# Attention of a trunk layer: full-row low products, inverse sums by two products, four heads' values together

## The chip, the cores and the metric

The kernel runs on one core of a Trainium2 chip. The metric is the device time of one execution in microseconds (us), as a median of runs. TensorE is called PE here (its weight loads PEld), VectorE DVE, ScalarE ACT, GpSimd POOL, SyncE SP.

## What is computed

The reference is a two-layer trunk for 512 latent tokens and 256 context tokens of 1024 features, followed by a second, larger block. The change touches only the attention of the trunk's layers: eight query heads of 64 features share two key and value heads, four query heads each. Cut to what matters here:

```python
def gqa_attend(qb, k, v):
    s = jnp.einsum('bqhgd,bkhd->bhgqk', qb, k, preferred_element_type=jnp.float32) * HEAD_DIM ** -0.5
    p = jax.nn.softmax(s, axis=-1)
    return jnp.einsum('bhgqk,bkhd->bqhgd', p.astype(v.dtype), v)

def trunk_layer(...):
    qc_, kc_, vc_ = attn_qkv(aqc, akc, avc, g_q, g_k)        # context: 256 tokens
    ql, kl, vl = attn_qkv(aq, ak, av, g_q, g_k)              # latent: 512 tokens
    k_all = jnp.concatenate([kc_, kl], axis=1)
    v_all = jnp.concatenate([vc_, vl], axis=1)
    ... latent_attention(ql, k_all, v_all) ...               # both layers
    ... context_attention(qc_, kc_, vc_) ...                 # first layer only
```

## The kernel before

Everything is float32. The large products run as three passes over float32r operands: each operand is split into a high part and a low rest, and high times high, high times low and low times high are added up in PSUM (`mm3`, L293 to L297). Weights stream in by SP's queue, and ACT, DVE and POOL make their two parts (L282, L284, L285).

The order of all instructions is set when the program is built: the kernel is written as straight code, and a scheduler of the framework interleaves it per engine by a timeline that it simulates. Each engine then runs its list in that order and waits on semaphores.

Attention is run three times: for the context in the first layer (4 blocks of 128 queries and four heads), and for the latent tokens in both layers (8 such blocks each). `keys` normalises the keys, turns them feature-major with PE and writes them into one tile `K`: the high parts of the two key heads on all 128 partitions (each head's 64 features twice, one copy above the other), and the low part of a head on one half of the partitions only (L871). `attend` then takes one head of one block after the other:

- `queries` (once a block): scaled and turned queries, four transposes into the bank `at`, then a tile `q` that holds the high part on one half of the partitions and the low part on the other (L920, L921).
- `scores`: for each set of keys a product on all 128 rows with the keys' high parts (L929), so that high and low part of the query are both covered, then a product on the 64 rows of the query's high half with the keys' low part (L930), and a maximum (L931). For the latent tokens there are two sets, 512 keys (bank `SL`) and 256 keys (bank `SC`), so two products on 64 rows for each head; for the context one set.
- `weights`: exponentials with their sums (L944), transposes of 128 columns each into `at` or the right half of the bank `op` (L947), copies to `PT` (L250 and L252).
- `values`, after every second head: products with 64 columns of the values, so that one head's result lies on the upper half of the partitions and the other's on the lower (L956). After the fourth head also the reciprocal of the sums (L962), four products that spread the inverse sums over 64 partitions each (L965, into `at`), a copy (L968) and two multiplications that write the output and free `op` (L970).

A float32 product shows as two records in the trace, a float32r product as one. Beside attention PE runs other work in the same stretches: the projections and the context's MLP (L295 to L297), the gated linear attention (`gla_out`, L705 to L744), pieces of the modulation (L450).

Of the kernel before, what the change touches and what calls it, by code (L numbers as in the profile page):

```python
# [7 lines left out]
LAG = 1  # L8
# [15 lines left out]
# groups of 256 columns of the scan's convolved part: keys, queries and values of two of its groups at a time  # L24
# [3 lines left out]
# ---------------------------------------------------------------- host side: layout and shape constants  # L28
# [5 lines left out]
def _pack(w, cols, kb=4):  # L34
    """[K, N] -> groups of 1024 rows and cols columns, each in contiguous loads of [128, kb*cols]."""
    K, N = w.shape
    return np.ascontiguousarray(
        w.reshape(K // 1024, 8 // kb, kb, 128, N // cols, cols).transpose(0, 4, 1, 3, 2, 5)
    ).reshape(-1, 128, kb * cols)


class Pieces:
    """Tiles side by side, sliced as one piece of memory; no slice reaches over an end."""
# [28 lines left out]
def _bands():  # L72
    """Windowed mean minus the token itself, as matrices over [token in, token out]."""
# [118 lines left out]
# ---------------------------------------------------------------- the kernel  # L192
class Kern:
    SHARED = {"const", "wraw", "whi", "wlo", "mod", "gs", "nv", "nr"} | {f"V{i}" for i in range(8)}
    # work space: tag -> count, of [128, 512]
    WORK1 = dict(E=2, K=2, Q=2, AT=1, QE=1, q=2, d=1, ab=1)
    WORK2 = dict(fa=3, fr=2, fu=2, fy=2, gG=3, gk=2, gm=2, dv=2, dk=2, dq=2, da=2, dn=2, dd=2, jy=2)
    # the tags of a normalisation's square, variance, root and product
# [21 lines left out]
    def w(self, tag, n=512, dt=F32):  # L220
        """Work space [128, n]."""
# [21 lines left out]
    # -- small helpers  # L243
# [12 lines left out]
    def split(self, src, hi, lo, f=None):  # L256
        """src = hi + lo exactly, both in float32r."""
        nc = self.nc
        nc.scalar.activation(hi, src, AF.Copy)
        nc.vector.tensor_tensor(lo, src, hi.bitcast(F32), op=ALU.subtract)  # L260

    def rsqrt(self, v, out, tmp):
        """out = v ** -0.5 of few columns: a first value from the exponent's bits and Newton's steps. v is kept."""
# [9 lines left out]
    # -- weights  # L273
    def whalf(self, name, i, n, kb, soon=True):
        """One load of a packed weight: its two float32r parts, [128, kb, n / kb]."""
# [12 lines left out]
    def wload(self, name, g, soon=True):  # L288
        """A group of 1024 rows and 256 columns, as a function of the block of rows."""
# [9 lines left out]
    def dense(self, name, groups, h, n, consume, halves=(0, 1), soon=True):  # L299
        """out^T [128 features, n tokens] per block of 128 columns of the weight; h per block of its rows."""  # L300
# [15 lines left out]
    def tokens(self, name, g, h, ntb, consume):  # L316
        """out [128 tokens, 256] for pairs of token blocks."""
# [13 lines left out]
    # -- parts of the tokens  # L331
    def parts(self, n, split=1):
        """Halves of the latent tokens, so that one half's normalisation runs beside the other half's products."""
# [3 lines left out]
    def cut(self, blocks, s):  # L337
        """A part of the tokens of blocks, or of pairs of blocks."""
        return [tuple(p[:, s] for p in b) if isinstance(b, tuple) else b[:, s] for b in blocks]

    def dense_parts(self, name, groups, h, n, consume, before, after, halves=(0, 1)):
        """As dense, with the first and the last groups done for one part of the tokens after the other."""
# [8 lines left out]
    # -- normalisation over features, feature-major  # L351
    def bank(self, n):
        """A bank of the work's own, outside the dense products' rotation."""
# [3 lines left out]
    def squares(self, x, n, tags, gains=None):  # L357
        """Means over the features of the squares of x, plus epsilon: token-major columns [128, n / 128]. With gains
        [128, 8, 2], as second columns the means of the squares times those."""
# [27 lines left out]
        # EPS v + mean: the second norm's variance over the first one's factor  # L387
# [4 lines left out]
    def root(self, v):  # L392
        """v ** -0.5"""
# [4 lines left out]
    def spread(self, r):  # L398
        """Columns [128 tokens, blocks] as a row over all partitions, [128, tokens]."""
# [7 lines left out]
    def norm_mod(self, x, n, gs, sh, hs, tags):  # L407
        """hs: pairs that take the two parts of the normalised blocks."""
# [12 lines left out]
    # -- modulation vectors  # L421
    def conditions(self, a, b):
        """silu of two vectors: [128, 8, 32], two columns and zeros."""
# [10 lines left out]
    def modulation(self, name, st, bias, part, bank="mm"):  # L434
        """One of the six vectors, feature-major [128, 8, 2] for both conditions: left to be done a piece at a time
        between other products. Four blocks of rows at a time, each in its own 32 columns of the array."""
# [32 lines left out]
    def flush(self):  # L469
        """Ends the pieces that were begun."""  # L470
# [3 lines left out]
    def modulation_v(self, name, st, bias, part, first=0):  # L474
        """The same for the first condition alone, by the vector engine."""
# [20 lines left out]
    def tick(self, n=1):  # L496
        """Does the next pieces of what was left for later."""
# [6 lines left out]
    def gain(self, mod, j, g):  # L504
        """(1 + scale) * gain for condition j."""
# [17 lines left out]
    def after(self, a, tile):  # L523
        """Has the loads into a tile wait for an array: they would take the place of more urgent ones."""
# [10 lines left out]
    # -- one layer of the first block  # L535
    def area(self, tag, w=8192):
        """A piece of memory, cut up by take()."""
        return self.t([128, w], tag)
# [4 lines left out]
    def blocks(self):  # L543
        """Eight blocks of [128, 512]: the latent residual, or others in its place."""
        return [self.t([128, 512], f"V{i}") for i in range(8)]

    def hpairs(self):
        """Eight pairs of [128, 512] in the three pieces that take a layer's input."""
# [7 lines left out]
    def ground(self):  # L556
        """The layer's larger arrays."""
        return Pieces([self.area("U0", 3072), self.area("U1", 2048), self.area("U2", 2048), self.area("U3", 1024)])

    def keep(self, out):  # L560
        """Takes token-major blocks as they are."""
# [5 lines left out]
    def dup(self, out, scale):  # L567
        """Takes token-major blocks of four heads and turns them feature-major, twice over the partitions."""
# [15 lines left out]
    def gla_proj(self, l, h, n, o):  # L584
        nc = self.nc
        # four blocks of rows at a time, each in its own 32 columns of the array; the gates' product adds them up
# [28 lines left out]
    # -- gated linear attention, both directions: partitions 0-63 forward, 64-127 backward  # L615
# [1304 lines left out]
```

## Time and profile before

| | |
|---|---|
| Median of 3 runs | 3656.49 us (3649.99 to 3657.73) |
| Span of the profiled execution, first to last instruction | 3646.2 us |
| PE busy in the span | 3414.7 us, 94% |
| DVE, ACT, POOL busy | 60%, 40%, 44% |
| Mean granted clock of PE | 0.956 of full |

The profiled execution has no time of its own beside its span; the median of the three timed runs lies 10.3 us above that span. Busy time of PE counts overlapping records once, and the ends of its records are modelled, so the pace of PE is read from the start of one product to the start of the next. A granted clock of 1.0 means 2.4 GHz, 0.5 means 1.2 GHz.

### The profile page before, as it was taken

How to read it: one execution, taken by the hardware profiler on the slowest of the kernel's cores; microseconds unless marked ns; L12 is line 12 of the kernel's file. 1: busy time of each engine (PE TensorE's matmuls, PEld its weight loads, DVE VectorE, ACT ScalarE, POOL GpSimd, SP SyncE). 2: the span in 40 equal slices, each digit the busy share in tenths (PEclk: the TensorE clock that was granted, in tenths of full speed). 3: DMA queues.
4: the chain of work that ended last, by engine and by line, in shares of the span. 5: the costliest groups of instructions: out<-in, count | busy, mean ns of one | idle time of the engine just before them, and what ended most of it. 6: DMA issues, size and time to landing. Idle time of an engine off the chain costs nothing. (4 is left out here: it accounts for less than half of the span.)

```text
span 3646.2 us, 55656 instructions
## 1 busy us (share of the span) xinstructions
PE 3414.7 (94%) x20714; PEld 2833.3 (78%) x20714; DVE 2174.3 (60%) x3724; ACT 1466.0 (40%) x2587; POOL 1601.3 (44%) x1370
## 2 busy tenths in 40 slices
PE   7999999989999999999999998998899998989998
PEld 5777788877788787677788776787898776788886
DVE  4844877457533358755633789768757767564233
ACT  4522765453222255632223655554233323254222
POOL 2522465542343235422344555446445545555433
PEclk9898999999999999999999999999999999989999
DMA  6344124635522220045522364456366666454222
GB/s 224 116 143 137 44 74 140 213 117 162 174 99 98 94 70 22 10 134 189 188 95 91 120 195 131 153 159 191 124 186 203 196 201 184 144 167 145 94 97 75
DMA packets 268414, 492.67 MB, mean 135 GB/s; under 512 B 44912, under 2 KB 129904, under 8 KB 267888
## 3 DMA queue, kind: packets, MB, share of 16 engines
q1 hardware_dynamic: 214128, 447.17, 38.3%
q10 hardware_dynamic: 54016, 41.95, 3.5%
q8 instruction: 163, 2.67, 0.3%
q14 instruction: 107, 0.88, 0.1%
HBM read 431.22 MB, written 57.80 MB: 134 GB/s over the span
## 5 line engine op out<-in xcount | busy, mean ns | idle before, releaser
L285 POOL TENSOR_TENSOR wlo<-wraw,whi 128x384 fp32r<-128x384 f32 (+1 forms) x503 | 736.1, 1464 | 1265.2 <-ACT whi L282 1178.0
L295 PE MATMUL mm<-h,whi 128*128 128x512 f32 (+1 forms) x2344 | 865.3, 372 | 38.1 <-ACT h L418 7.4
L282 ACT ACTIVATE whi<-wraw 128x1024 fp32r<-128x1024 f32 x503 | 530.9, 1056 | 866.2 <-PE mm L296 648.2
L296 PE MATMUL mm<-h,whi 128*128 128x512 f32 (+1 forms) x2344 | 857.6, 366 | 14.2 <-DVE h L419 11.7
L284 DVE TENSOR_TENSOR wlo<-wraw,whi 128x640 fp32r<-128x640 f32 (+1 forms) x503 | 481.7, 958 | 636.3 <-ACT whi L282 629.8
L297 PE MATMUL mm<-h,wlo 128*128 128x512 f32 (+1 forms) x2344 | 841.0, 365 | 6.0 <-DVE wlo L284 5.9
L295 PEld LDWEIGHTS mm<-h,whi 128*128 128x128 f32 x2344 | 448.7, 192 | 124.2 <-ACT whi L282 11.5
L296 PEld LDWEIGHTS mm<-h,whi 128*128 128x128 f32 x2344 | 449.8, 192 | 93.4 <-DVE h L419 20.9
L297 PEld LDWEIGHTS mm<-h,wlo 128*128 128x128 f32 x2344 | 448.4, 192 | 80.7 <-DVE wlo L284 8.8
L296 PE MATMUL mm<-wlo,h 128*128 128x256 f32 x1200 | 353.5, 296 | 32.5 <-DVE wlo L284 27.7
L295 PE MATMUL mm<-whi,h 128*128 128x256 f32 x1200 | 353.2, 297 | 10.7 <-ACT whi L282 9.8
L297 PE MATMUL mm<-whi,h 128*128 128x256 f32 x1200 | 350.0, 293 | 0.0
L296 PEld LDWEIGHTS mm<-wlo,h 128*128 128x128 f32 x1200 | 235.2, 196 | 43.1 <-DVE wlo L284 32.5
L295 PEld LDWEIGHTS mm<-whi,h 128*128 128x128 f32 x1200 | 234.7, 197 | 27.7 <-ACT whi L282 12.5
L297 PEld LDWEIGHTS mm<-whi,h 128*128 128x128 f32 x1200 | 235.2, 196 | 17.2 <-issue 13.7
L295 PE MATMUL mm<-U,whi 128*128 128x512 f32 (+1 forms) x608 | 228.6, 379 | 5.8 <-DVE V L1080 5.8
L296 PE MATMUL mm<-U,whi 128*128 128x512 f32 (+1 forms) x608 | 227.5, 376 | 0.9 <-DVE U L260 0.9
L297 PE MATMUL mm<-U,wlo 128*128 128x512 f32 (+1 forms) x608 | 223.6, 376 | 0.0
L487 DVE SCALAR_TENSOR_TENSOR AT<-mraw,cst,AT 128x512 f32<-128x512 f32 x140 | 119.2, 851 | 88.6 <-DMA mraw<-in_w_ada 52.7
L295 PE MATMUL mm<-big,whi 128*128 128x512 f32 x384 | 155.0, 405 | 5.6 <-ACT whi L282 2.3
L296 PE MATMUL mm<-big,whi 128*128 128x512 f32 x384 | 153.6, 400 | 0.0
L297 PE MATMUL mm<-big,wlo 128*128 128x512 f32 x384 | 150.9, 401 | 0.0
(580 smaller groups left out, 5980.3 us busy)
## 6 DMA issues: line engine op xcount, KB each, us to landing
wraw<-in_w_in SPq DMA_DIRECT2D x166, 512.0 KB, 3.5
wraw<-in_w_up SPq DMA_DIRECT2D x96, 512.0 KB, 3.3
wraw<-in_w_down SPq DMA_DIRECT2D x96, 512.0 KB, 3.3
mraw<-in_w_mod SPq DMA_DIRECT2D x96, 256.0 KB, 3.0
mraw<-in_w_ada SPq DMA_DIRECT2D x96, 256.0 KB, 2.8
wraw<-in_w_out SPq DMA_DIRECT2D x40, 512.0 KB, 3.3
wraw<-in_w_mlp_up SPq DMA_DIRECT2D x40, 512.0 KB, 3.3
mraw<-in_w_late SPq DMA_DIRECT2D x64, 256.0 KB, 2.8
```

The costliest lines, as they stand in the source:

```text
L282: nc.scalar.activation(hi, raw, AF.Copy)
L284: nc.vector.tensor_tensor(lo[:, :c], raw[:, :c], hi[:, :c].bitcast(F32), op=ALU.subtract)
L285: nc.gpsimd.tensor_tensor(lo[:, c:], raw[:, c:], hi[:, c:].bitcast(F32), op=ALU.subtract)
L295: nc.tensor.matmul(out, lh, rh, start=start, stop=False)
L296: nc.tensor.matmul(out, lh, rl, start=False, stop=False)
L297: nc.tensor.matmul(out, ll, rh, start=False, stop=stop)
L487: nc.vector.scalar_tensor_tensor(acc, raw, st[:, k, 0:1], acc, op0=ALU.mult, op1=ALU.add)
```

## The change

Four edits in `keys` and `attend`, and one in how the program is set up:

1. `K` has four slots instead of three. The low parts of both key heads are now written on all 128 partitions by one subtraction of [128, 2, 256] in place of two of [64, 256].
2. The product with the keys' low part runs on all 128 rows. It thus adds the product of the query's low part with the keys' low part too.
3. `values` is called once a block, after the fourth head, for all four heads. `PT` has six buffers instead of three, since four heads' turned exponentials are now held.
4. The inverse sums are first spread by ACT into a tile [128, 4, 64]; then two products with 128 columns take the place of four with 64.
5. The scratch memory set aside for dynamic DMAs is 1024 bytes.

```diff
-        K = self.t([128, 3, n], f"K{n}", 1, F32R)
+        K = self.t([128, 4, n], f"K{n}", 1, F32R)
...
-                for g in range(2):
-                    s = slice(g * 64, g * 64 + 64)
-                    nc.vector.tensor_tensor(K[s, 2, t], tp[s, g], K[s, g, t].bitcast(F32), op=ALU.subtract)
-        return [(K[:, g], K[g * 64:g * 64 + 64, 2]) for g in range(2)], [x[:, 128:] for x in o["kv"]]
+                nc.vector.tensor_tensor(K[:, 2:, t], tp, K[:, :2, t].bitcast(F32), op=ALU.subtract)
+        return [(K[:, g], K[:, 2 + g]) for g in range(2)], [x[:, 128:] for x in o["kv"]]
...
-            his, qh = halves(g)[0], q[:, hh * 128:(hh + 1) * 128]
+            qh = q[:, hh * 128:(hh + 1) * 128]
             for i, (kk, _, c) in reversed(list(enumerate(ksets))):
                 hi, lo = kk[g]
                 nc.tensor.matmul(at[i], qh, hi, start=True, stop=False)
-                nc.tensor.matmul(at[i], qh[his], lo, start=False, stop=True)
+                nc.tensor.matmul(at[i], qh, lo, start=False, stop=True)
...
-            pt = self.t([128, 768], "PT", 3)[:, :nk]
+            pt = self.t([128, 768], "PT", 6)[:, :nk]
...
-        def values(g, qb, pr, x, pts, op):
-            for b, v in enumerate(vals):
-                for j in range(2):
-                    nc.tensor.matmul(op[j * 64:j * 64 + 64, pr * 128:(pr + 1) * 128], v[:, g * 64:(g + 1) * 64],
-                                     pts[j][:, b * 128:(b + 1) * 128], start=(b == 0), stop=(b == len(vals) - 1))
-            if pr == 0:
-                return
+        def values(g, qb, x, pts, op):
+            for pr in range(2):
+                for b, v in enumerate(vals):
+                    for j in range(2):
+                        nc.tensor.matmul(op[j * 64:j * 64 + 64, pr * 128:(pr + 1) * 128], v[:, g * 64:(g + 1) * 64],
+                                         pts[pr * 2 + j][:, b * 128:(b + 1) * 128], start=(b == 0),
+                                         stop=(b == len(vals) - 1))
...
-            for h in range(4):
-                nc.tensor.matmul(r[h % 2 * 64:h % 2 * 64 + 64, h // 2 * 128:(h // 2 + 1) * 128],
-                                 x[:, 4, h:h + 1].to_broadcast([128, 64]), self.ident, start=True, stop=True)
+            inv = self.t([128, 4, 64], "inv")
+            nc.scalar.activation(inv, x[:, 4].unsqueeze(2).to_broadcast([128, 4, 64]), AF.Copy)
+            for i in range(2):
+                nc.tensor.matmul(r[:, i * 128:(i + 1) * 128], inv[:, 2 * i:2 * i + 2].rearrange("p h e -> p (h e)"),
+                                 self.ident, start=True, stop=True)
...
-                if hh % 2:
-                    values(*blocks[b], hh // 2, stats[b], (pts[n - LAG - 1], pts[n - LAG]), opt[b])
+                if hh == 3:
+                    values(*blocks[b], stats[b], [pts[b * 4 + j] for j in range(4)], opt[b])
...
-    nc = bacc.Bacc("TRN2", target_bir_lowering=False, num_devices=1)
+    nc = bacc.Bacc("TRN2", target_bir_lowering=False, num_devices=1, dynamic_dma_scratch_size=1024)
```

How the built order moves. PE, second layer, a block of latent queries between its second and fourth head (rows of a line are instruction, output <- inputs with buffer numbers, output size). Before:

```order
L956 MATMUL op_13141<-PT_13185,V_1880_11533 64x128
L947 MATMUL op_13141<-const_69,P_13254 128x128 x2
L929 MATMUL SL_12588<-K_1996_12518,q_13118 128x512
L930 MATMUL SL_12588<-K_1996_12518,q_13118 128x512
L715 MATMUL sm_14098<-U_1855_11449,U_1854_11448 128x128 x4
L929 MATMUL SC_12590<-K_1406_8545,q_13118 128x256
L930 MATMUL SC_12590<-K_1406_8545,q_13118 128x256
L947 MATMUL at_13260<-const_69,P_13254 128x128 x4
L956 MATMUL op_13141<-PT_13205,vc_8558 64x128
L956 MATMUL op_13141<-PT_13253,vc_8558 64x128
L956 MATMUL op_13141<-PT_13205,vc_8558 64x128
```

In the changed kernel L955 is the values' product (L956 before), L927 and L928 are the scores' (L929 and L930), L945 the transposes (L947):

```order
L955 MATMUL op_13123<-PT_13179,V_1892_11529 64x128
L955 MATMUL op_13123<-PT_13199,vc_8554 64x128
L955 MATMUL op_13123<-PT_13235,vc_8554 64x128
L955 MATMUL op_13123<-PT_13199,vc_8554 64x128
L955 MATMUL op_13123<-PT_13235,vc_8554 64x128
L955 MATMUL op_13123<-PT_13199,V_1891_11528 64x128
L927 MATMUL SC_12584<-K_1418_8542,q_13100 128x256
L928 MATMUL SC_12584<-K_1418_8542,q_13100 128x256
L715 MATMUL sm_14092<-U_1867_11445,U_1866_11444 128x128 x4
L945 MATMUL at_13263<-const_69,P_13257 128x128 x4
L955 MATMUL op_13123<-PT_13235,V_1891_11528 64x128
```

The first two heads' values no longer stand apart, with scores and transposes between them and the next two heads'; they come straight ahead of the other two, and the scheduler breaks the sequence a few products later.

PE, the same layer, from a block's last product of values to the first transposes of the next block into `op`. Before:

```order
L956 MATMUL op_13141<-PT_13253,V_1880_11533 64x128
L721 MATMUL sm_14098<-Q_14092,K_14091 64x64 x7
L929 MATMUL SL_12589<-K_1996_12518,q_13118 128x512
L930 MATMUL SL_12589<-K_1996_12518,q_13118 128x512
L721 MATMUL sm_14098<-Q_14092,K_14091 64x64
L929 MATMUL SC_12590<-K_1406_8545,q_13118 128x256
L930 MATMUL SC_12590<-K_1406_8545,q_13118 128x256
L965 MATMUL at_13301<-const_69,ast_13098 64x128 x4
L721 MATMUL sm_14098<-Q_14113,K_14112 32x32 x16
L947 MATMUL at_13324<-const_69,P_13318 128x128 x4
L947 MATMUL op_13273<-const_69,P_13275 128x128 x2
```

In the changed kernel:

```order
L955 MATMUL op_13123<-PT_13235,V_1892_11529 64x128
L927 MATMUL SL_12583<-K_2008_12514,q_13100 128x512
L928 MATMUL SL_12583<-K_2008_12514,q_13100 128x512
L721 MATMUL sm_14092<-Q_14086,K_14085 64x64 x5
L927 MATMUL SC_12584<-K_1418_8542,q_13100 128x256
L928 MATMUL SC_12584<-K_1418_8542,q_13100 128x256
L721 MATMUL sm_14092<-Q_14086,K_14085 64x64 x3
L965 MATMUL at_13295<-const_69,inv_13296 128x128 x2
L721 MATMUL sm_14092<-Q_14107,K_14106 32x32 x16
L945 MATMUL at_13318<-const_69,P_13312 128x128 x4
L945 MATMUL op_13255<-const_69,P_13257 128x128 x2
```

The spread of the inverse sums (L965 in both) has two products of 128 columns in place of four of 64, and stands at the same place between the products of `gla_out` (L721); the next block's transposes into `op` follow it as before.

ACT, the same block: the copy of the fourth head's transposes (PT), exponentials (P) and what stands around them. Before:

```order
L920 ACTIVATE q_13250<-at_13245 128x512
L749 ACTIVATE E_14086<-U_1854_11448 128x256
L944 ACTIVATE P_13275,ast_13230<-SC_12590,ast_13230 128x256
L250 ACTIVATE PT_13253<-op_13141 128x256
L706 ACTIVATE E_14090<-E_14090 128x4x64
L707 ACTIVATE E_14090<-E_14090 128x4x64
L250 ACTIVATE PT_13253<-at_13260 128x512
```

In the changed kernel, with the new copy L963:

```order
L942 ACTIVATE P_13257,ast_13212<-SL_12582,ast_13212 128x512
L250 ACTIVATE PT_13235<-op_13123 128x256
L963 ACTIVATE inv_13296<-ast_13080 128x256
L942 ACTIVATE P_13257,ast_13212<-SC_12584,ast_13212 128x256
L250 ACTIVATE U_1866_11444<-sm_14070 128x256
L736 ACTIVATE QE_14210<-U_1868_11446 64x512
L738 ACTIVATE QE_14210<-U_1868_11446,tot_12429 64x128 x4
L749 ACTIVATE E_14080<-U_1866_11444 128x256
```

The new copy stands behind the fourth head's first copy, some sixteen instructions ahead of the copy L968 that closes the block; the other instructions keep their order but for single places.

## Rows read from the trace of the kernel before

**Rows 1.** The page: busy us, share of the span and instructions of each engine.
```profile
PE 3414.7 (94%) x20714; PEld 2833.3 (78%) x20714; DVE 2174.3 (60%) x3724; ACT 1466.0 (40%) x2587; POOL 1601.3 (44%) x1370
```
**Rows 2.** Busy time by stage; columns as the first line says.
```profile
core 0: us, PE busy (x) PEld busy (x) DVE busy (x) ACT busy (x) POOL busy (x), PEclk, DMA share, GB/s
125.00:290.00 165.00, 158.19 (x1246) 125.70 (x1242) 91.87 (x222) 54.99 (x136) 53.17 (x51) 0.89 0.42 133
350.00:440.00 90.00, 83.79 (x590) 67.30 (x590) 76.03 (x154) 67.78 (x150) 37.17 (x32) 0.87 0.20 66
350.00:600.00 250.00, 242.26 (x1985) 199.79 (x1987) 201.70 (x382) 165.41 (x394) 136.57 (x127) 0.95 0.21 68
1345.00:1565.00 220.00, 203.63 (x1588) 157.45 (x1587) 165.05 (x340) 127.91 (x330) 102.42 (x99) 0.91 0.08 25
```
**Rows 3.** Line L930 alone: count, ns min/median/max, first and last start, forms.
```profile
L930 PE MATMUL SL<-K,q x80: 379/498/792, 131.1 to 1545.2; 64*128 64x512 f32 x64, 64*128 64x256 f32 x16
L930 PE MATMUL SC<-K,q x64: 379/381/579, 350.7 to 1546.9; 64*128 64x256 f32 x64
```
**Rows 4.** PE in time: start, us, line, output<-inputs, rows*columns of the array.
```profile
571.16 0.40 PE L929 MATMUL SL<-K,q 128*128 128x512 f32 x1
571.49 0.50 PE L930 MATMUL SL<-K,q 64*128 64x512 f32 x1
571.92 0.39 PE L295 MATMUL mm<-h,whi 128*128 128x256 f32 x1
572.14 0.28 PE L296 MATMUL mm<-h,whi 128*128 128x256 f32 x1
572.26 0.28 PE L297 MATMUL mm<-h,wlo 128*128 128x256 f32 x1
...
572.49 0.28 PE L929 MATMUL SC<-K,q 128*128 128x256 f32 x1
572.70 0.38 PE L930 MATMUL SC<-K,q 64*128 64x256 f32 x1
573.01 0.39 PE L296 MATMUL mm<-h,whi 128*128 128x256 f32 x1
573.24 0.28 PE L297 MATMUL mm<-h,wlo 128*128 128x256 f32 x1
```
**Rows 5.** PE in time around one spread of inverse sums.
```profile
552.57 0.28 PE L297 MATMUL mm<-h,wlo 128*128 128x256 f32 x1
552.78 0.66 PE L965 MATMUL at<-const,ast 128*64 128x128 f32 x8
553.37 0.39 PE L295 MATMUL mm<-h,whi 128*128 128x256 f32 x1
553.60 0.28 PE L296 MATMUL mm<-h,whi 128*128 128x256 f32 x1
```
**Rows 6.** PE in time around one sequence of two heads' values.
```profile
508.99 0.28 PE L297 MATMUL mm<-h,wlo 128*128 128x256 f32 x1
509.20 0.66 PE L956 MATMUL op<-PT,vc 128*64 128x128 f32 x8
509.69 1.04 PE L956 MATMUL op<-PT,V 128*64 128x128 f32 x16
510.66 0.44 PE L947 MATMUL op<-const,P 128*128 128x128 f32 x2
```
**Rows 7.** Lines L968 (ACT) and L871 (DVE): count, ns min/median/max.
```profile
L968 ACT ACTIVATE oo<-at x20: 365/384/386, 155.1 to 1561.6; 128x256 f32<-128x256 f32 x20
...
L871 DVE TENSOR_TENSOR K<-at,K x12: 403/418/428, 103.3 to 1345.2; 64x256 fp32r<-64x256 f32 x12
```
**Rows 8.** What PE waited for, 125 to 290: us in total, times, longest.
```profile
PE SC L450 <- DMA mraw<-in_w_mod: 5.4, 5, 1.8
```
**Rows 9.** The same from 1440 to 1565 us.
```profile
PE op L947 <- DVE ma L970: 1.5, 2, 1.2
```
**Rows 10.** Weight loads from 533 to 600 us: busy us, mean ns.
```profile
L296 PEld LDWEIGHTS mm<-h,whi 128*128 128x128 f32 x66 | 12.4, 188 | 0.8 <-issue 0.4
```

## Prediction

> **What bounds the kernel now.** I read the page first: PE is busy for 94% of the span, the next engine for 60% [rows 1]. The change touches attention only, so the stages of attention decide, not the mean. They stand in the busy time by stage [rows 2]: the context's attention (125 to 290 us), the first layer's latent attention (350 to 600) and the second's (1345 to 1565). PE is busy for 96%, 97% and 93% of them, DVE for 56%, 81% and 75%, ACT for less. In all three other work of PE stands between the heads, so that PE rarely lacks something to do: what is taken from PE shortens the stage until another engine is late.
>
> A busy PE need not be a working PE, so I then read PE in order of time, from start to start. Between products on 128 rows and 128 columns the pace is 0.12 us for 256 columns (572.14 to 572.26) [rows 4]. Around each product on 64 rows it breaks. For 512 keys: from the high product at 571.16 over the low one at 571.49 and the next two dense products, the second of which starts at 572.14, pass 0.98 us. By the pace these three products take 0.24 + 0.24 + 0.12 = 0.60 us (512 columns taken as twice 256, an estimate). So 0.38 us go to entering and leaving the 64-row form. For 256 keys: 572.49 to 573.24 is 0.75 us for three products of 0.12, so 0.39 us. The loss doesn't grow with the columns, so it is a price of the change of form. The same shows with half of the columns: two dense products and one spread of inverse sums take 552.57 to 553.60, 1.03 us [rows 5].
>
> **The low products (144 of them).** L930 has 80 products into SL and 64 into SC [rows 3]; in the built order each stands alone between products of another form, and in the changed order none is left. The columns stay the same, and a product on 128 rows takes the pace above. So 144 x 0.39 = 56 us of PE time are freed, 6 in the context's stage and 25 in each latent stage. Some of them ran at the lower clock, where the price is higher (L930's longest record is 792 ns against a median of 498 [rows 3]); I leave that out of the sum.
>
> A rule of the Trainium skill speaks against this edit: by "TensorE: Matmul & The Clock Gate" (Part 3, The mechanism) a weight load overlaps with products under way only where its row group differs, and then a load for all 128 rows would have to stand alone. Here the trace disagrees: loads of full form last 188 ns in the mean [rows 10], yet products of full form start every 0.12 us.
>
> **The inverse sums.** In the built order their column products form 21 sequences for 20 blocks; none is left. From the 1.03 us of [rows 5] go 0.24 for the two dense products; the new spread is two float32 products of 128 columns, four records, each at most the 0.12 of a 256-column one, so at most 0.48. That leaves 0.31 us a block, 21 x 0.31 = 6.5 us. The new copy on ACT is a [128, 256] activation; the nearest row is L968 with 384 ns [rows 7], so 20 x 0.38 = 7.7 us of ACT. ACT is busy for 66% and 58% of the latent stages, and in the built order the copy stands some sixteen instructions ahead of the one that ends the block, so I cost it at nothing; without that cover it would be 7.7 us.
>
> **The values.** In the built order their sequences fall from 52 to 42, not to 20, because the scheduler breaks them. A sequence of 24 products takes 1.67 us from the dense product before it to the product after it [rows 6]. Sixteen of its products, eight pairs, take at most 0.97 us (509.69 to 510.66), so at most 0.12 a pair; with 0.12 for the dense product, 0.11 us is the least that entering and leaving cost, and 0.38 as for the rows the most. I take 0.25, nearer to the sum's middle: 10 x 0.25 = 2.5 us (1 to 4). Other short sequences of `gla_out` and of the pooling are cut up by four more in the new order: minus 4 x 0.3 = 1 us.
>
> **Edits with one answer.** The subtractions of the keys become six of twice the columns instead of twelve of 418 ns [rows 7]: between 2.5 us less and nothing on DVE, ahead of the heads, at nothing. `PT` and the scratch memory move no work; every large load is issued on SP. The queues of SP and POOL keep their instructions, single ones change places inside the attention stages.
>
> **The sum.** 56 + 6.5 + 2.5 - 1 = 64 us of PE time are freed: 8 in the first stage, 28 in each of the latent ones. How much of it the end sees:
> - Context, 8 us: PE already waits 5.4 us there for loads of modulation weights [rows 8], which come at their own pace. I take 5.5.
> - First layer, 28 us: in its first 90 us DVE is already busy for 84% (76.0 of 90.0) [rows 2]. If DVE can be had to 90% (an estimate), that stretch shrinks to 84.5 us, 5.5 of the 11 us freed there. The other 17.5 I take in full: together 23.
> - Second layer, 28 us: DVE would stand at 165 / 192 = 86%. But PE lies idle for 16 of the 220 us, waiting for the gated linear attention and for block ends [rows 2, 9], and those waits will grow. I take four fifths: 23.
>
> That is 51.5, rounded to 52. The span goes from 3646.2 to 3594 us. The median lies 10.3 us above the span of the profiled execution; I keep that distance: 3604 us.
>
> **Rivals.**
> 1. *DVE and POOL take over.* If DVE can't be had above the 84% it reaches now, the first layer's stage ends at 201.7 / 0.84 = 240 us, 10 us saved; with 12 in the second and 3 in the context's stage 25 us: 3631. For it: DVE is the second engine, and engines run their lists in order. Against it: part of DVE's present waits is for the score products themselves, which come earlier.
> 2. *The clock helps too.* The mean granted clocks of 0.89, 0.95 and 0.91 [rows 2] are about 36 + 25 + 40 = 100 us at 1.2 GHz. By the ratio of 792 to 498 ns [rows 3] they would take 63 us at 2.4 GHz. If closer products keep the clock up for most of it, the gain is up to 52 + 37 = 89 us: 3567. Against it: waits for other engines grow as well. The reverse, more time at 1.2 GHz, is in the range.
> 3. *The change doesn't do what it says*: the gap belongs to the score products in another way than by their rows, and stays. Then 8 us of the other edits are left, 7 of them seen: 3649. Against it: the same gap stands around the column products, and never between two dense ones.
> 4. *Weight loads of full form stand alone.* 144 x 0.188 = 27 us are given back; of the 37 left some four fifths are seen, 30: 3626. The rule quoted above would bring this; [rows 4, 10] speak against it.
> 5. *Slower, by the block's end.* `op` holds both the outputs and the next block's transposes, and now all values stand between the fourth head and its release. If nothing else ran there, a latent block's end would cost 24 pairs of 0.12, the spread 0.48, two copies of 0.38 and two multiplications (at most the same 0.38 each): 4.9 us. For the 16 latent blocks and 4 smaller ones (half) that is 88 us, 36 more than the 52 gained: 3692. It decides from 52 / 20 = 2.6 us a block. Against it: now PE waits twice for that release in the second layer's last 125 us, 1.2 us at the longest [rows 9], and scores and the products of L721 stand in between in the new order too.
>
> **How the numbers follow.** The forecast (3580 to 3618) has 0.61, rival 1 has 0.20, rival 2 beyond 3580 has 0.08, rival 3 has 0.05, rival 4 has 0.02, rival 5 has 0.04. The range 3580 to 3634 leaves out rivals 2, 3 and 5 and the worst of rival 1, some 0.19 together. It contains the bounds of the values' price and the copy on ACT. A measurement of this kernel can tell about 0.2%, 7 us. Faster by more than that: forecast, rivals 1, 2, 4 and two fifths of rival 3, 0.93; within it: 0.03; slower: 0.04.
>
> **What would show it.** After a score product with the low keys, the next product of full form should start at the pace, with no gap in front and behind; three products as in [rows 4] should take 0.60 and 0.36 us. The spread should cost under 0.5 us. The latent stages should be about 227 and 197 us long, DVE's share in them near 89% and 84%, and everything behind them as before, only earlier. Rival 1 would show in PE's waits for DVE and POOL, rival 5 in waits of L947 into `op` for L970 of over 2.6 us a block, rival 2 in granted clocks near 1.0. If the dense stages outside attention change in length, the sum has missed something.

## The result and the profile after

The changed kernel takes 3615.4 us (median of 4 runs, 3614.4 to 3616.6) against 3657.1 us of the kernel before on the same chip: a ratio of 0.9896, 95% interval 0.9876 to 0.9916. The gain of 41.7 us is ten less than the forecast gain of 52, and the time lies in the forecast's own range of 3580 to 3618 us.

The page of the changed kernel: busy us, share of the span and instructions of each engine, to set against [rows 1].

```profile
PE 3361.3 (93%) x20634; PEld 2820.5 (78%) x20634; DVE 2163.8 (60%) x3718; ACT 1469.5 (41%) x2607; POOL 1591.8 (44%) x1370
```

PE's busy time fell by 53 us and the span only from 3646.2 to 3614.7. PE in order of time in the changed kernel, to set against [rows 4] and [rows 5]; L927 and L928 are the scores with the keys' high and low parts, L965 the spread of the inverse sums:

```profile
495.67 0.28 PE L295 MATMUL mm<-h,whi 128*128 128x256 f32 x1
495.78 0.40 PE L927 MATMUL SL<-K,q 128*128 128x512 f32 x1
496.01 0.40 PE L928 MATMUL SL<-K,q 128*128 128x512 f32 x1
496.25 0.28 PE L296 MATMUL mm<-h,whi 128*128 128x256 f32 x1
496.37 0.28 PE L297 MATMUL mm<-h,wlo 128*128 128x256 f32 x1
...
536.82 0.28 PE L296 MATMUL mm<-h,whi 128*128 128x256 f32 x1
536.93 0.61 PE L965 MATMUL at<-const,inv 128*128 128x128 f32 x4
537.30 0.37 PE L297 MATMUL mm<-h,wlo 128*128 128x256 f32 x1
537.51 0.28 PE L295 MATMUL mm<-h,whi 128*128 128x256 f32 x1
...
545.83 0.28 PE L927 MATMUL SC<-K,q 128*128 128x256 f32 x1
545.95 0.28 PE L928 MATMUL SC<-K,q 128*128 128x256 f32 x1
546.07 0.28 PE L297 MATMUL mm<-h,wlo 128*128 128x256 f32 x1
546.19 0.28 PE L295 MATMUL mm<-h,whi 128*128 128x256 f32 x1
```

For 512 keys three products now take 495.78 to 496.37 = 0.59 us, where [rows 4] show 0.98 and the forecast said 0.60. For 256 keys it is 545.83 to 546.19 = 0.36 us, as forecast, against 0.75. Two dense products and a spread take 536.82 to 537.51 = 0.69 us against 1.03 in [rows 5] and 0.72 forecast.

Where the time went is read by stage, with the same pieces of work in both kernels: a stage begins and ends where ACT starts to split the same weights (L282). Busy time by stage in the kernel before, in the order context's attention, first latent attention, the rest of the first layer, second latent attention:

```profile
core 0: us, PE busy (x) PEld busy (x) DVE busy (x) ACT busy (x) POOL busy (x), PEclk, DMA share, GB/s
99.00:327.00 228.00, 217.85 (x1687) 172.75 (x1686) 122.70 (x300) 72.75 (x169) 77.89 (x77) 0.89 0.41 130
327.00:624.00 297.00, 285.94 (x2351) 238.57 (x2350) 233.70 (x446) 187.83 (x436) 156.91 (x146) 0.96 0.26 85
624.00:1052.00 428.00, 405.62 (x2346) 339.80 (x2345) 236.11 (x374) 155.16 (x222) 165.83 (x127) 0.96 0.51 163
1321.00:1583.00 262.00, 241.16 (x1813) 191.34 (x1814) 188.54 (x386) 144.97 (x357) 118.49 (x111) 0.91 0.11 35
```

The same stages of the changed kernel, same columns:

```profile
101.00:317.00 216.00, 203.67 (x1681) 165.91 (x1680) 122.49 (x306) 75.03 (x175) 78.32 (x79) 0.94 0.42 137
317.00:600.00 283.00, 263.67 (x2304) 235.46 (x2303) 227.09 (x432) 188.07 (x442) 156.48 (x144) 0.95 0.27 87
600.00:1039.00 439.00, 413.09 (x2354) 345.20 (x2353) 240.15 (x380) 155.09 (x221) 165.88 (x127) 0.94 0.50 160
1307.00:1555.00 248.00, 215.39 (x1780) 182.83 (x1781) 186.53 (x384) 146.85 (x366) 116.95 (x111) 0.94 0.12 37
```

| stage | length | PE busy | PE idle (length less busy) | forecast of the length |
|---|---|---|---|---|
| context's attention | -12.0 | -14.2 | +2.2 | -5.5 |
| first latent attention | -14.0 | -22.3 | +8.3 | -23 |
| rest of the first layer | +11.0 | +7.5 | +3.5 | 0 |
| second latent attention | -14.0 | -25.8 | +11.8 | -23 |
| everything else | -2.5 | | | 0 |

Three things stand there. PE's work shrank in the attention stages by 62 us. That looks like the 64 forecast, but by luck: the context's stage lost 14.2 where 8 were forecast, at a higher clock (0.94 against 0.89), and the two latent stages only 22.3 and 25.8 where 28 each were forecast. Of these 48 us, 20 came back as idle time of PE. The context's stage gained more than forecast. And a stage in which the change alters practically nothing became 11 us longer. These differences come from one execution of each kernel; the experiments add a second profile of before and two of the changed kernel.

### The profile page after: what moved, and what is told of

The parts are those of the page before. It is cut to its first block, busy times and chain, and to the rows that moved or that the text cites. A ratio compares the mean times of both kernels' runs of the same rounds, so it can differ in the third digit from the quotient of the medians.

```text
span 3614.7 us, 55539 instructions
## 1 busy us (share of the span) xinstructions
PE 3361.3 (93%) x20634; PEld 2820.5 (78%) x20634; DVE 2163.8 (60%) x3718; ACT 1469.5 (41%) x2607; POOL 1591.8 (44%) x1370
## 5 line engine op out<-in xcount | busy, mean ns | idle before, releaser
L282 ACT ACTIVATE whi<-wraw 128x1024 fp32r<-128x1024 f32 x503 | 530.9, 1055 | 868.9 <-PE mm L296 655.4
L296 PE MATMUL mm<-h,whi 128*128 128x512 f32 (+1 forms) x2344 | 856.4, 366 | 12.8 <-DVE h L419 10.8
L296 PEld LDWEIGHTS mm<-wlo,h 128*128 128x128 f32 x1200 | 235.4, 196 | 41.7 <-DVE wlo L284 32.1
```

The source lines that it names most:

```text
L282: nc.scalar.activation(hi, raw, AF.Copy)
L296: nc.tensor.matmul(out, lh, rl, start=False, stop=False)
```

## The experiments

All kernels here carry the smaller scratch memory (edit 5); the fifth run measures it alone.

**The low products alone** (edits 1 and 2).

```diff
-                nc.tensor.matmul(at[i], qh[his], lo, start=False, stop=True)
+                nc.tensor.matmul(at[i], qh, lo, start=False, stop=True)
```

> The kernel before with the low score products on all 128 rows alone; values and inverse sums as before. Theory A (each entry into the 64-row form costs 0.39 us of PE, 56 of the 64 us freed are the low products'): 56/64 of the 42 us gained, so 37 us faster than before, about 3620 us, ratio 0.990. Rival B (the gain comes from the block's end, the gap at the low products stays in another guise): under 10 us faster, about 3649 us.

3621.6 us, ratio 0.9904 (0.9885 to 0.9923): the low products carry 33 us of the gain.

**Everything but the low products** (edits 3 and 4).

```diff
+            inv = self.t([128, 4, 64], "inv")
+            nc.scalar.activation(inv, x[:, 4].unsqueeze(2).to_broadcast([128, 4, 64]), AF.Copy)
...
+                if hh == 3:
+                    values(*blocks[b], stats[b], [pts[b * 4 + j] for j in range(4)], opt[b])
```

> The changed kernel with the low products back on 64 rows: only the inverse sums by two full products and the four heads' values in one sequence. Theory A: 9 of 64 us freed, so 4 to 8 us faster than before, 3649 to 3653 us. Rival B: 30 us or more faster, about 3625 us. Rival C (values held to the block's end cost more than they give): slower than before, over 3657 us.

3650.6 us against 3655.1, ratio 0.9985 (0.9964 to 1.0005): 4.5 us less, and the interval contains no change.

**Low products and inverse sums, values as before** (edits 1, 2 and 4).

```diff
-                if hh == 3:
-                    values(*blocks[b], stats[b], [pts[b * 4 + j] for j in range(4)], opt[b])
+                if hh % 2:
+                    values(*blocks[b], hh // 2, stats[b], (pts[n - LAG - 1], pts[n - LAG]), opt[b])
```

> The changed kernel with the values again after every second head and three PT buffers. Theory A: the values' edit frees 2.5 us of PE, so 0 to 4 us slower than the changed kernel, 3615 to 3619 us. Rival C (values held to the block's end delay the next block's transposes into op): 5 to 15 us faster than the changed kernel, 3600 to 3610 us.

3615.0 us, 0.9892 (0.9870 to 0.9915), the same as the changed kernel: the gathered values are worth nothing that can be measured. Against the low products alone it is 6.6 us less, the 6.5 us forecast for the inverse sums, though the intervals overlap.

**The changed kernel again**, without an edit, on the chip of the three runs above.

> The changed kernel once more, for a second profile. In the first profile 12 to 14 us that attention had gained were lost again between the first layer's attention and the end of its MLP (725 to 990 us), where the clock stood at 1.2 GHz for some 51 us against 31 us before. Theory D (the order and waits of that stage set it): again about 51 us there, and about 3615 us in all. Rival E (it falls by chance): another amount, by over 7 us, and a time that follows it at about half.

3614.9 us, 0.9887 (0.9868 to 0.9905). The stage behind the first attention is again longer than before:

```profile
599.50:1036.60 437.10, 410.65 (x2354) 343.85 (x2353) 239.75 (x379) 155.26 (x222) 165.32 (x127) 0.95 0.50 161
```

By the clock's records in the traces, PE ran at 1.2 GHz for 44 us of this stage, against 51 us in the first profile of the changed kernel and 31 in that of the kernel before. That is 7 us less than the first time, on the border between theories D and E.

**The kernel before with the smaller scratch memory** (edit 5).

```diff
-    nc = bacc.Bacc("TRN2", target_bir_lowering=False, num_devices=1)
+    nc = bacc.Bacc("TRN2", target_bir_lowering=False, num_devices=1, dynamic_dma_scratch_size=1024)
```

> The kernel before with the smaller scratch memory alone; all engines' orders are those of before. Same time as before (3655 us, within 7 us). Its profile is a second look at the kernel before: theory D (the changed order makes the clock fall more often in the first layer's MLP, 725 to 990 us) expects about 31 us at 1.2 GHz and 427 us for that stage as in the first profile of before; rival E (chance, run by run) expects another amount, by over 7 us, and a stage longer or shorter by about half of the difference.

3653.0 us against 3652.9, 1.0005 (0.9986 to 1.0024): no difference. It is thus a second profile of the kernel before; its four stages in the same order:

```profile
101.00:339.60 238.60, 227.47 (x1693) 180.85 (x1692) 124.24 (x301) 73.89 (x170) 77.77 (x77) 0.85 0.37 124
339.60:636.50 296.90, 285.85 (x2352) 238.54 (x2351) 234.04 (x447) 187.59 (x437) 157.40 (x146) 0.96 0.25 86
636.50:1060.50 424.00, 401.85 (x2340) 337.83 (x2339) 235.76 (x374) 154.79 (x221) 167.07 (x127) 0.97 0.50 164
1329.00:1585.00 256.00, 231.19 (x1814) 184.08 (x1815) 190.38 (x386) 144.96 (x358) 120.19 (x111) 0.95 0.11 36
```

The length of the first latent stage repeats to 0.1 us; the context's stage and the second latent one differ by 11 and 6 us, the longer one each time at the lower granted clock (0.85 against 0.89, 0.91 against 0.95). The stage behind the first attention has 27 us at 1.2 GHz and 424 us, near the 31 and 427 that theory D asked for.

**More changes of form in the kernel before.** The scores of 512 keys are made in two halves, high, low, high, low: the columns stay the same, and 64 more visits of the 64-row form come in.

```diff
-                nc.tensor.matmul(at[i], qh, hi, start=True, stop=False)
-                nc.tensor.matmul(at[i], qh[his], lo, start=False, stop=True)
+                for a in range(0, c, 256):
+                    nc.tensor.matmul(at[i][:, a:a + 256], qh, hi[:, a:a + 256], start=True, stop=False)
+                    nc.tensor.matmul(at[i][:, a:a + 256], qh[his], lo[:, a:a + 256], start=False, stop=True)
```

> The kernel before, with the scores of the 512 latent keys done in two halves of 256 columns: high, low (64 rows), high, low. The columns are the same, 128 more products, and 64 more entries into the 64-row form. Theory A (a price of 0.39 us for each entry): 25 us more PE time, of which two thirds are seen, so about 17 us slower than before, 3672 us. Rival (the price belongs to the columns or to the sum in PSUM): within 5 us of before.

3680.9 us, 1.0088 (1.0060 to 1.0117): 28 us more, 0.44 us a visit, so the whole price of 64 x 0.39 = 25 us reaches the end, and not two thirds of it as expected. PE in order of time in that kernel (L930 high, L931 low):

```profile
571.98 0.36 PE L930 MATMUL SL<-K,q 128*128 128x256 f32 x1
572.28 0.38 PE L931 MATMUL SL<-K,q 64*128 64x256 f32 x1
572.59 0.38 PE L930 MATMUL SL<-K,q 128*128 128x256 f32 x1
572.90 0.38 PE L931 MATMUL SL<-K,q 64*128 64x256 f32 x1
```

Each product starts 0.31 us after the last, where full forms of 256 columns keep 0.12: entering costs 0.19 us, and leaving as much.

**The kernel before, and the changed kernel, without the maxima.** The exponentials take the scores divided by 64 in place of the scores less their maximum; DVE's reductions fall away. The edit in the kernel before (the changed one has the same):

```diff
-                nc.vector.tensor_reduce(x[:, i, hh:hh + 1], at[i], axis=AX.X, op=ALU.max, negate=True)
-            if len(ksets) == 2:
-                nc.vector.tensor_tensor(x[:, 0, hh:hh + 1], x[:, 0, hh:hh + 1], x[:, 1, hh:hh + 1], op=ALU.min)
...
-                nc.scalar.activation(e, S[i], AF.Exp, bias=x[:, 0, hh:hh + 1], accum_out=x[:, 2 + i, hh:hh + 1])
+                nc.scalar.activation(e, S[i], AF.Exp, scale=1.0 / 64, accum_out=x[:, 2 + i, hh:hh + 1])
```

> The kernel before without the maxima: the reductions of the scores and their minimum are left out, the exponentials are taken of scores divided by 64 so that they stay finite (another function than softmax of the scores). That takes some 100 us from DVE in attention and one step from the chain scores, maximum, exponential, transposes. Theory F (before the change PE bounds the stages): under 12 us faster than before, over 3643 us.

> The changed kernel without the maxima, in the same way. Theory F (with PE relieved, its new waits are for DVE and the chain over the maxima): at least 20 us faster than the changed kernel, under 3595 us, more than e7 gains on before. Rival G (PE is still the bound, the missing gain went to the clock alone): as much as e7 gains, within 5 us.

Before: 3647.3 us, 0.9989 (0.9967 to 1.0010), nothing that can be measured. Changed: 3590.9 us, 0.9845 (0.9816 to 0.9874), 24 us less than the changed kernel with them by the medians, which are of different chips; by the ratios (0.9887 and 0.9896 with the maxima) it is 15 to 19 us. The two latent stages of the changed kernel without maxima, and the second one of the kernel before without them:

```profile
319.00:598.00 279.00, 260.02 (x2341) 234.59 (x2340) 196.37 (x327) 181.71 (x441) 160.94 (x146) 0.98 0.29 96
1297.00:1532.00 235.00, 212.99 (x1781) 183.41 (x1782) 153.59 (x288) 140.08 (x366) 116.65 (x111) 0.94 0.12 39
```

```profile
1324.00:1579.00 255.00, 237.33 (x1813) 186.56 (x1814) 149.60 (x290) 140.02 (x358) 116.62 (x111) 0.93 0.11 36
```

In the second layer PE's idle time falls with the maxima from 32.6 to 22.0 us in the changed kernel, and from 20.8 (24.8 in the second profile) to 17.7 in the kernel before. The stage is shorter by 13 us in the changed kernel and by 1 to 7 in the kernel before: there the way over DVE holds PE up mostly since PE became faster. In the first layer PE is idle for 19.0 us against 19.3, although DVE has 31 us less to do: neither DVE's load nor the way over the maximum is what holds PE there. The second layer's 13 us are the larger part of the gain, the first layer's stage has 4, and what is left isn't placed by one profile.

**The changed kernel with finer scores, with other copies, and with both.** Finer scores are the halves above, now all on 128 rows. The copies to `PT` that DVE makes go to ACT.

```diff
-                self.copy(pt[:, done:done + c], tp, "a" if c == NL or hh % 2 else "v")
+                self.copy(pt[:, done:done + c], tp, "a")
```

> The changed kernel with the same cut of the latent scores into two halves of 256 columns as in e6: the same 128 additional products, but all on 128 rows, so no additional change of form. Theory A (the price is the form's): within 8 us of the changed kernel (3615 us), where e6 lost 28. Rival (the price of e6 is that of more products and of the order): 20 us or more slower, over 3635 us. It is also a third look at the first layer's MLP behind a changed attention: theory D expects over 40 us at 1.2 GHz and over 433 us for that stage, rival E something else.

> The changed kernel with all copies of turned exponentials on ACT: 40 copies of 0.42 us leave DVE, 40 of 0.38 come to ACT. If DVE's load is what PE now waits for, 5 to 10 us faster than the changed kernel (3605 to 3610 us); if it is the chain through ACT (maximum, exponential, transposes, copy), 0 to 10 us slower (3615 to 3625 us).

> The changed kernel with both alterations of the two runs before: scores of 512 keys in two halves of 256 columns (3598.0 us alone) and all copies to PT on ACT (3604.5 us alone), against 3615 us for the changed kernel. If the two gains have separate causes (finer products for the one, less load on DVE for the other), they add: 3615 - 17 - 11 = 3587 us, 3580 to 3594. If both only set PE's order and clock anew, the sum is no better than the better of them: 3596 to 3606 us. If the copies crowd ACT once the scores come earlier, over 3606 us.

Finer: 3598.0 us, 0.9860 (0.9839 to 0.9882). Copies: 3604.5 us, 0.9873 (0.9856 to 0.9889). Both: 3607.0 us, 0.9885 (0.9860 to 0.9910). Beside the changed kernel's 0.9887 and 0.9896, all intervals overlap. Finer scores came out 17 us faster by the medians where within 8 us was expected, and the kernel with both lies 1 us above the bound that was set for crowded copies on ACT, too little to tell. That finer scores cost nothing here, where they cost 28 us in the kernel before, is clear: the price belongs to the form and not to one more product. The stage behind the first attention took 430 us with finer scores, 34 of them at 1.2 GHz; theory D had asked for over 433 and over 40. A gain by either edit is not shown, since the kernel with both doesn't have it. The lowest time of a kernel that does all the work is thus 3598 us, but it isn't shown to beat the change.

**The changed kernel a third time**, without an edit.

> The changed kernel once more, for a third profile of the first layer's stage behind attention. If the change itself lowers the clock there, that stage again has 44 us or more at 1.2 GHz and is 436 us long or longer; if it was chance, it lies anywhere between 27 us and 51 us, and a value under 35 us (430 us or less) would show so.

3613.6 us (one run), and the stage in question lies between what the two theories asked for, with 38 us at 1.2 GHz:

```profile
599.80:1033.70 433.90, 407.57 (x2354) 341.55 (x2353) 241.70 (x379) 155.28 (x222) 166.34 (x127) 0.96 0.49 162
```

## Why the prediction was right, and where its sizes were off

**The price of the form** was right in size and cause. The rows of the changed kernel (0.39 us less for three products, at 512 keys as at 256) and the kernel before with 64 visits more (0.44 us each) agree with the 0.39 taken; of the 56 us that 144 visits cost by that price, 33 reached the end. Rival 3, that the gap belongs to something else, is out.

**Rival 4** is out: products of full form with new weights for each keep the pace of 0.12 us around L927 and L928, and 27 us given back would show as 0.19 us in front of each. The rule of the Trainium skill from which it came ("TensorE: Matmul & The Clock Gate", Part 3, The mechanism) doesn't describe these rows.

**Inverse sums and values**: 6.6 us between two medians against 6.5 forecast, with intervals that overlap, so that it agrees but isn't shown; nothing measurable against 2.5. The new copy on ACT lasts longer than the 0.38 us taken for it, and the waits for it come to 0.6 us in all. Line L963 of the changed kernel (count, ns min/median/max, first and last start, forms), and who waited for it (us, times):

```profile
L963 ACT ACTIVATE inv<-ast x20: 398/415/451, 145.3 to 1525.6; 128x256 f32<-128x256 f32 x20
...
  PEld mm L1035: 0.4, 1
  PEld op L955: 0.2, 1
```

**What the latent stages let the end see** is the term that was mis-sized. Forecast were 28 us of PE time freed in each, and 23 of them, four fifths, seen at the end. Both sizes were too large. By PE's busy time 24 us were freed in the first and 20 in the second, between the means of all five profiles. The first stage became 14 us shorter (297 and 297 in the two of before; 283, 282.5 and 282.4 in the three of the changed kernel). The second gave 14 in the pair of profiles, or 10 between the means of all five (262 and 256; 248, 249 and 250). So 60% and 50% of what was freed reached the end.

The limit that the forecast set in the first stage, DVE at 90%, was meant for the first 90 us of attention, which end with the scores of the twelfth head. In the changed kernel this piece is (columns as in the tables by stage above):

```profile
333.00:428.00 95.00, 82.25 (x622) 72.03 (x621) 75.44 (x156) 73.49 (x162) 38.11 (x33) 0.86 0.24 78
```

It didn't shrink; more of PE's other work stands in it now (622 records against 590 in [rows 2]). DVE is busy for 79% of it, where it was 84%, and PE is idle for 12.8 us against 6.2. So DVE never came near its limit. What PE waited for in the first latent stage of the changed kernel, 317 to 600 us (us in total, times, longest; `sm` is the bank of the gated linear attention's products):

```profile
PE op L945 <- ACT P L942: 2.9, 2, 2.4
PE SL L927 <- ACT P L942: 2.1, 1, 2.1
PE sm L733 <- DVE AT L734: 1.9, 2, 1.1
PE sm L629 <- DVE gst L252: 1.4, 1, 1.4
PE sm L733 <- POOL Q L729: 1.1, 2, 0.8
```

The same in the second latent stage, 1307 to 1555 us:

```profile
PE mm L296 <- DVE wlo L284: 3.9, 2, 3.2
PE at L945 <- ACT oo L968: 2.8, 3, 1.3
...
PE at L945 <- DVE q L919: 2.3, 1, 2.3
PE op L945 <- DVE PT L252: 2.1, 4, 1.0
...
PE op L945 <- DVE ma L970: 0.9, 2, 0.6
...
PE op L945 <- DVE V L970: 0.7, 1, 0.7
```

The longest wait, for the split of a weight, was there before the change too (3.8 us, 3.2 the longest), so it is the growth that counts. Added up by the bank that PE was about to write, us:

| stage, bank | before, two profiles | changed, three profiles |
|---|---|---|
| first, attention (`SL`, `SC`, `at`, `op`) | 5.7; 5.7 | 9.0; 10.1; 9.3 |
| first, `sm` | 1.5; 1.5 | 6.0; 6.8; 6.8 |
| first, `mm` (projections) | 2.9; 2.9 | 3.9; 4.9; 4.4 |
| second, attention | 5.5; 6.5 | 16.0; 16.7; 16.4 |
| second, `sm` | 5.5; 8.0 | 7.6; 8.2; 6.9 |
| second, `mm` | 9.9; 10.0 | 9.1; 7.4; 9.0 |

In the second stage the growth is attention's alone, 10 us. No single wait makes it up; it is the chain of one head (scores, maximum, exponentials, transposes, copy), of which now one link and now another is late, and without the maxima attention's waits fall from 16.0 to 8.3 us. DVE, with a quarter of its time free, still holds PE up there, because the order leaves it no time between two links. In the first stage attention's waits grew by 4 us and those of the gated linear attention by 5, and without the maxima the two fall only from 9.0 to 7.9 and from 6.0 to 5.0 us. What holds PE there isn't shown; it is not DVE's load. Rival 1 was thus half right: others take over a part, but by their place in the chain and not by being full, and the run without maxima shows it for DVE in the second layer.

**Rival 5** did not come: L970 into `op` costs 1.6 us in three waits, 0.7 us at the longest, where 2.6 us a block were needed. A little of the block's end shows at `at`, where the spread and the copy L968 stand: 2.8 us in three waits. In the kernel before, 1321 to 1583 us, it was:

```profile
PE at L947 <- ACT oo L968: 1.0, 2, 0.5
```

**The context's stage** gave 12 us, between the means of all five profiles 17, where 5.5 were forecast. Two steps failed. The loads of modulation weights don't hold the stage: the wait of [rows 8], 5.4 us, is down to this in the changed kernel, in the same stretch:

```profile
PE SC L450 <- DMA mraw<-in_w_mod: 0.6, 1, 0.6
```

Other waits came in their place, and PE's idle time grew by 2 us in all. The second step is the clock. At a mean clock c a stage of t us has about 2 (1 - c) t us at 1.2 GHz, which is 50 and 72 us in the two profiles of before and 26 in the changed kernel. In this stage the five kernels with the old low products have clocks of 0.84 to 0.92, the nine with the new ones 0.89 to 0.96. One of the nine, the changed kernel without maxima, has the 0.89 of the kernel before:

```profile
99.00:319.00 220.00, 206.92 (x1671) 168.94 (x1670) 118.93 (x282) 72.38 (x173) 76.01 (x77) 0.89 0.40 133
```

At this clock it took 8 us less than before, all that the forecast had freed. So by this one profile the rest of the 12 to 17 us came with the clock, as rival 2 describes, though it isn't shown that closer products are what kept the clock up. It came in this stage alone: the second latent stage had 0.91 in one profile of before but 0.95 in the other, against 0.94. Over the whole span the granted clock is 0.956 and 0.957 in the two profiles of before and 0.959, 0.959 and 0.962 in the three of the changed kernel. Rival 2 had 0.08 for the whole kernel.

**The stage behind the first attention** was to stay as it was. It is 11 us longer in the pair of profiles, with 51 us at 1.2 GHz against 31; its length goes with the clock in the profiles taken:

| kernel | length, us | granted clock |
|---|---|---|
| before; with smaller scratch | 428; 424 | 0.96; 0.97 |
| everything but the low products | 435 | 0.95 |
| before with more changes of form; without maxima | 435; 430 | 0.95; 0.96 |
| changed, three times | 439; 437; 434 | 0.94; 0.95; 0.96 |
| low products alone; with the inverse sums | 426; 432 | 0.96; 0.96 |
| changed without maxima; finer; copies; both | 431; 430; 439; 435 | 0.96; 0.96; 0.95; 0.96 |

Kernels with the old low products have 430 us in the mean, those with the new ones 434, and both kinds spread over 11 us or more. Three profiles of the changed kernel all lie above two of before, but kernels of either kind lie on the other side. So the stage is longer where its clock is lower, and whether the change itself lowers the clock there, by what it leaves behind, stays open (the means leave some 3 us for it, the pair of profiles 11).

**The median and the span.** The forecast carried the 10.3 us between span and median along as a distance. It is none: the profiled execution of the changed kernel took 3616.6 us for a span of 3614.7, 1.9 us more. The other eight came from a profiled execution under the median of the kernel before, whose single runs went from 3631 to 3671 us across the chips. The step cancelled in the gain, but it is why the two profiles differ by 31.5 us and the medians by 41.7.

Between the two spans the forecast had 20 us too much (51.5 against 31.5): 18 in the latent stages and 11 in the stage behind the first attention, while the context's stage gave back 6.5 and all else 2.5. The medians leave ten of these twenty, since the profiled execution of before lay some 8 us under the median. That the forecast came this close is thus in part luck: the clock in the context's stage, which it didn't count on, made up for a part of what the latent stages failed to give.

## What to carry to other kernels

Where one engine is busy for 95%, look for the starts of its instructions that break the pace: going to another form and back cost 0.39 us here, at 256 columns as at 512, and filling the idle rows with work cost nothing. Then count only half to six tenths of the time taken from the busy engine, where it feeds a chain through the others and comes back to it; this is what two stages gave here. With time gone from PE, other links of the chain came late, though their engines were idle for a fifth or more of the stage. And take two profiles of the kernel before for every stage on which a sum rests, since stages of the same program differed by 6 to 11 us with the granted clock.

## What the runs showed of the hardware

- A product on 64 of 128 rows between products on all rows costs 0.38 to 0.39 us at 2.4 GHz, for 256 columns as for 512; where the two forms alternate at 256 columns, each change costs 0.19 us. The Trainium skill, "TensorEngine Tiling (Array Packing)", Key Properties, says that changing the tiling mode drains TensorE; the gap of 0.19 us at each change agrees with that and gives the price.
- With 64 more of these visits the whole price reached the end (28 us against 25), while of the 56 us taken away 33 did: what was added to the bound engine counted in full here, what was removed didn't.
- Single runs of the kernel before spread over 1%, and its stages differ between two executions by 10 us at granted clocks that differ by 0.04. Every difference of a stage that is under 10 us and goes with the clock needs more than one profile.
